# Value products of block 1's attention: both heads stationary on the full array instead of one head per half of the columns

## The chip, the cores and the metric

One core of one Trainium2 chip runs the whole program. The metric is device time in microseconds. The engines are TensorE (PE in the profile; its weight loads are listed apart as PEld), VectorE (DVE), ScalarE (ACT), GpSimd (POOL), SyncE (SP, which issues most transfers) and the DMA engines. [...]

## The reference, cut to what matters

Two transformer blocks over 1024 tokens of width 1024. The change lies in the first block's attention: 8 heads of width 64, a mixture of dilated windows.

```python
s = jnp.einsum('brnqhd,brnkhd->brnhqk', qb, kw) + bias
p = jnp.exp(s - m);  den = jnp.sum(p, -1)
o = jnp.einsum('brnhqk,brnkhd->brnqhd', p / den, vw)   # the value products
...
O = sum_i softmax(lse)_i * o_i                          # over the dilations
mix = concat(O, sgu) @ w_out
```

## The kernel before, in words

**The stage.** Block 1 has a projection part, then one `flow(gating(), attention())` call, then the output projection (`wo`) and the feed-forward layers. `flow` is a planner: it runs Python generators and decides in which order they emit their instructions, by estimated times. `gating()` is the dense stream: it makes 4 x 4 tiles `zv` and `zu` (48 matmuls of 256 columns each) and 8 tiles `mixp`. `attention()` handles head pairs j = 0 to 3: project q and k of the pair (`qk_proj`, tiles `q_p` and `k_p`, put into the dense stream), the scores of both heads (`att_scores`, tiles `spA`, `spB`), and then the value products of the pair in two halves of the tokens (`att_values(j, 0)` and `att_values(j, 1)`). The values of a pair are spawned beside the projections and scores of the next pair. A second scheduler then orders the emitted instructions on each engine by priority and by which buffers are free; each engine runs its list strictly in that order.

**A value tile.** `att_values(j, u)` makes the 128 x 512 result `oT`: 64 features of each of the two heads on the partitions, 512 tokens in the columns. It has eight steps n. In each, POOL scales the weights of both heads (`src`), PE transposes them into one bank `pt` (4 transposes of 128 columns), ACT or DVE copies the bank to `P` in SBUF, and one step later PE multiplies values by `P`. In steps 0 to 3 a step owns 128 consecutive tokens, in steps 4 to 7 every fourth token. In each step there are two halves m of the keys and two heads e, four matmuls in all:

```python
o, v = oT[ps, 128 * q:128 * q + 128], vA[:, 4 * u + q + m, ps]     # ps: 64 partitions of head e
PE.matmul(o, v, P[:, m, e, :], ...)
```

The stationary operand is 128 keys x 64 features, so a matmul takes half of the array's columns; the head picks the half. All are plain float32, which the hardware runs in two passes: each matmul of these shows as two records in the trace (the dense matmuls are float32r, one record each). At the end ACT copies `oT` to `ot` in SBUF (L689) and sends it to DRAM, from where `split_at` reads it for the output projection.

**Banks.** PSUM is split into two pools of four banks: `pg` (tag "g") for the dense stream (`zv`, `zu`, `mixp`, `q_p`, `k_p`), `psd` (tag "s") for the scores, the transposes `pt` and, before, `oT`.

Of the kernel before, what the change touches and what calls it, by code (L numbers as in the profile page):

```python
# [9 lines left out]
F32 = mybir.dt.float32  # L10
# [107 lines left out]
def tile_hybrid_two_blocks(ctx, tc, A, out, dbg=None, stop=None):  # L118
    nc = tc.nc
    dbg = dbg or {}  # L120
    PE, ACT, DVE, POOL, SP = nc.tensor, nc.scalar, nc.vector, nc.gpsimd, nc.sync
# [5 lines left out]
    pg = ctx.enter_context(tc.tile_pool(name="pg", bufs=PGB, space=PSUM))  # L127
    psd = ctx.enter_context(tc.tile_pool(name="psd", bufs=8 - PGB, space=PSUM))
# [528 lines left out]

    def att_values(j, u):

        sts = [st_of[2 * j], st_of[2 * j + 1]]  # L660
        vA, vB = vAB_of[j]
        oT = psd.tile([128, 512], F32, tag="s", name=f"oT{j}{u}")
        for n in range(9):
            if n < 8:
                i = 4 * u + n % 4
                pt = psd.tile([128, 2, 2, 128], F32, tag="s", name=f"pt{j}{u}{n}")
                for e in range(2):
                    a, b, mdA, mdB = sts[e]
                    src, md = (a[u][:, n, :], mdA) if n < 4 else (b[u][:, n - 4, :], mdB)
                    wt = md[:, 4 + i % 4 // 2, 2 * (i % 2) + i // 4:2 * (i % 2) + i // 4 + 1]  # L670
                    POOL.tensor_scalar(src, src, wt, 0.0, op0=ALU.mult, op1=ALU.add)
                    for m in range(2):
                        PE.transpose(pt[:, m, e, :], src[:, 128 * m:128 * m + 128], ident)
                P_ = p1.tile([128, 2, 2, 128], F32, tag="PT", name=f"PT{j}{u}{n}", bufs=3)
                (DVE.tensor_copy if n % 2 else ACT.copy)(P_, pt)
            if n:
                q = n - 1
                for m in range(2):
                    for e in range(2):
                        ps = slice(64 * e, 64 * e + 64)  # L680
                        if q < 4:
                            o, v = oT[ps, 128 * q:128 * q + 128], vA[:, 4 * u + q + m, ps]
                        else:
                            o, v = oT[ps, q - 4:512:4], vB[:, 4 * m + q - 4, ps]
                        PE.matmul(o, v, P[:, m, e, :], start=q == 0 and m == 0, stop=q == 7 and m == 1)
            P = P_
            yield 4 * MM, LT["vt"]
        ot = p1.tile([128, 512], F32, tag="PT", name=f"ot{j}{u}", bufs=3)
        ACT.copy(ot, oT)  # L689
        ACT.dma_start(at_d[u][j], ot)  # L690

    def attention():
        vs = []

        def first(j):
            yield 0, LT["ex"]
            yield from att_values(j, 0)

        def second(j, before):
            yield Join(before)  # L700
            yield from att_values(j, 1)

        for j in range(4):
            yield Job(qk_proj(j))
            yield 0, LT["qk"]
            for e in range(2):
                if vs:
                    yield Join(vs.pop(0))
                if e:
                    load_v(j)  # L710
                yield from att_scores(2 * j + e)
            a = yield Spawn(first(j))
            vs = [a, (yield Spawn(second(j, a)))]
        yield Join(vs[1])
# [797 lines left out]
```

## Time and profile before

| | |
|---|---|
| Time, median of 3 runs | 2614.74 us (2614.11 to 2618.09) |
| The profiled execution: time, span | 2613.16 us, 2611.2 us |
| PE busy | 2447.1 us, 94% of the span |
| PE weight loads busy | 1999.4 us, 77% |
| DVE, ACT, POOL busy | 57%, 47%, 9% |
| Mean granted PE clock, share of full | 0.971 |
| Value products (L685) on PE | 512 records, 164.1 to 429.1 us |

The share of PE is an average over the whole program, most of which is feed-forward layers. The value products of block 1 lie between 164 and 430 us, six tiles interleaved with the dense stream and two (the last pair) after it has ended. In the trace a matmul's duration contains the time that it takes to run through the array, so neighbours overlap; what a matmul costs the engine is read from the distance between starts.

### The profile page before, as it was taken

The page shows a single profiled execution, that of the slowest core. Times are in us where ns is not written, and L with a number is a line of the kernel's source. Part 1 is how long each engine was busy: PE and PEld are TensorE (multiplying, and loading weights), DVE is VectorE, ACT ScalarE, POOL GpSimd, SP SyncE. Part 2 cuts the span into 40 slices and gives each one's busy share as a digit, 9 for nine tenths or more (in the row PEclk, how much of TensorE's full clock was granted, in tenths as well). Part 3 has the DMA queues.
Part 4 walks back from the last instruction along what each step waited for, and adds up shares of the span by engine and source line. Part 5 has one row for each costly group of instructions (what it writes and reads, how often), then busy time and mean ns, then how long its engine had stood idle before and what let it go on. Part 6 is the DMA issues. An engine that isn't in the chain of part 4 may idle for free. (4 is left out here: it accounts for less than half of the span.)

```text
span 2611.2 us, 32731 instructions
## 1 busy us (share of the span) xinstructions
PE 2447.1 (94%) x12024; PEld 1999.4 (77%) x12024; DVE 1490.4 (57%) x2755; ACT 1215.4 (47%) x2160; POOL 241.5 (9%) x356
## 2 busy tenths in 40 slices
PE   8999999999999999589999999878889999799997
PEld 8867778778788788467888878667668887688886
DVE  3346444566653469476443157989996554533436
ACT  5345554463333363255545373366755443633332
POOL 1034212100000000000000000122200000100002
PEclk9999999999999999789999999989899999899998
DMA  6412114489886676346558657522222225633332
GB/s 181 120 46 64 42 30 114 161 282 325 292 269 202 218 215 223 129 138 192 165 163 273 196 158 219 173 91 81 73 81 81 81 69 164 227 97 97 97 97 73
DMA packets 330784, 391.64 MB, mean 150 GB/s; under 512 B 42273, under 2 KB 227889, under 8 KB 330624
## 3 DMA queue, kind: packets, MB, share of 16 engines
q1 hardware_dynamic: 327216, 385.11, 47.1%
q10 hardware_dynamic: 3408, 4.46, 0.5%
q8 instruction: 94, 1.54, 0.2%
q14 instruction: 66, 0.54, 0.1%
HBM read 312.44 MB, written 80.73 MB: 151 GB/s over the span
## 5 line engine op out<-in xcount | busy, mean ns | idle before, releaser
L147 PE MATMUL fb_p<-h4h,fb_w_h 128*128 128x512 f32 x512 | 205.9, 403 | 13.0 <-ACT h4h L841 8.7
L148 PE MATMUL fa_p<-h2l,fa_w_h 128*128 128x512 f32 x512 | 204.5, 399 | 0.0
L149 PE MATMUL fa_p<-h2h,fa_w_l 128*128 128x512 f32 x512 | 203.2, 397 | 0.8 <-DMA fa_w_l<-fa_w_d 0.8
L148 PE MATMUL fb_p<-h4l,fb_w_h 128*128 128x512 f32 x512 | 203.9, 399 | 0.0
L147 PE MATMUL fa_p<-h2h,fa_w_h 128*128 128x512 f32 x512 | 203.6, 398 | 0.0
L149 PE MATMUL fb_p<-h4h,fb_w_l 128*128 128x512 f32 x512 | 203.2, 397 | 0.0
L1079 DVE SCALAR_TENSOR_TENSOR y<-glu,cw,y 128x512 f32<-128x512 f32 x240 | 180.1, 790 | 1.0
L176 ACT CAST fb_w_h<-fb_w_r 128x1024 fp32r<-128x1024 f32 x64 | 67.2, 1050 | 144.0 <-PE fb1o_p L149 74.1
L147 PEld LDWEIGHTS fb_p<-h4h,fb_w_h 128*128 128x128 f32 x512 | 97.7, 191 | 34.3 <-ACT h4h L841 8.9
L1189 ACT ACTIVATE junk<-sc,cand 128x768 bf16<-128x768 f32 (+2 forms) x93 | 86.9, 934 | 62.4 <-DVE cand L1187 60.5
L148 PEld LDWEIGHTS fb_p<-h4l,fb_w_h 128*128 128x128 f32 x512 | 97.8, 191 | 20.9 <-DVE h4l L842 0.3
L149 PEld LDWEIGHTS fb_p<-h4h,fb_w_l 128*128 128x128 f32 x512 | 97.5, 190 | 20.6
L148 PEld LDWEIGHTS fa_p<-h2l,fa_w_h 128*128 128x128 f32 x512 | 96.7, 189 | 21.4 <-issue 0.9
L147 PEld LDWEIGHTS fa_p<-h2h,fa_w_h 128*128 128x128 f32 x512 | 96.3, 188 | 21.8 <-ACT fa0o_w_h L176 0.9
L149 PEld LDWEIGHTS fa_p<-h2h,fa_w_l 128*128 128x128 f32 x512 | 96.7, 189 | 21.0 <-DMA fa_w_l<-fa_w_d 1.3
L177 DVE TENSOR_TENSOR fb_w_l<-fb_w_r,fb_w_h 128x1024 fp32r<-128x1024 f32 x53 | 64.9, 1224 | 82.5 <-ACT fb_w_h L176 82.4
L1131 PE MATMUL ip<-kT,qi 128*128 128x384 f32 (+3 forms) x160 | 60.6, 421 | 51.9 <-DMA qi<-qiT_d 35.8
L1277 DVE TENSOR_TENSOR PL<-pt,PT 128x512 fp32r<-128x512 f32 (+1 forms) x80 | 50.8, 636 | 73.5 <-ACT PT L1276 73.2
L176 ACT CAST fa_w_h<-fa_w_r 128x1024 fp32r<-128x1024 f32 x32 | 33.7, 1054 | 118.4 <-PE fa0o_p L149 77.8
L1131 PEld LDWEIGHTS ip<-kT,qi 128*128 128x128 f32 x160 | 33.7, 218 | 66.7 <-DMA qi<-qiT_d 33.7
L1168 DVE TENSOR_SCALAR_CACHE_REDUCE jk<-sc,cand 128x640 bf16<-128x640 f32 (+2 forms) x93 | 81.6, 877 | 2.2
L177 DVE TENSOR_TENSOR fb1o_w_l<-fb1o_w_r,fb1o_w_h 128x1024 fp32r<-128x1024 f32 x28 | 34.3, 1225 | 83.9 <-ACT fb1o_w_h L176 83.9
(1511 smaller groups left out, 7113.4 us busy)
## 6 DMA issues: line engine op xcount, KB each, us to landing
fa_w_r<-in_w_ff_dram SPq DMA_DIRECT2D x64, 512.0 KB
fb_w_r<-in_w_up_dram SPq DMA_DIRECT2D x64, 512.0 KB
ada_w<-in_w_ada_dram SPq DMA_DIRECT2D x48, 512.0 KB
fa_w_d<-fa_w_l SPq DMA_DIRECT2D x32, 512.0 KB
fa0o_w_r<-in_w_ff_dram SPq DMA_DIRECT2D x32, 512.0 KB
fa0o_w_d<-fa0o_w_l SPq DMA_DIRECT2D x32, 512.0 KB
fa_w_l<-fa_w_d SPq DMA_DIRECT2D x32, 512.0 KB
fa1o_w_r<-in_w_ff_dram SPq DMA_DIRECT2D x32, 512.0 KB
```

The costliest lines, as they stand in the source:

```text
L147: PE.matmul(out_, lh, rh, start=first, stop=False)
L148: PE.matmul(out_, lh, rl, start=False, stop=False)
L149: PE.matmul(out_, ll, rh, start=False, stop=last)
L176: ACT.copy(hi, raw)
L177: eng.tensor_tensor(lo, raw, hi.bitcast(F32), op=ALU.subtract)
L1079: DVE.scalar_tensor_tensor(y, g, w, y, op0=ALU.mult, op1=ALU.add)
L1131: PE.matmul(p, q[:, z, 128 * j:128 * j + 128], kT[:, g, c0:c0 + m], start=z == 0, stop=z == 1)
L1168: DVE.tensor_scalar(jk[:, :ss[e].shape[-1]], ss[e], thr, 0.0, op0=op, op1=ALU.add, accum_out=cnt[:, e:e + 1])
L1189: ACT.activation(junk[:, :ss[e].shape[-1]], ss[e], AF.Sign, bias=cand[:, e:e + 1].bitcast(F32), accum_out=cnt[:, e:e + 1])
L1277: DVE.tensor_tensor(tl[:, :kk], pt[:, :kk], th[:, :kk].bitcast(F32), op=ALU.subtract)
```

## The change

`oT` becomes two banks from `pg`, each 128 x 2 x 256: partitions for the features of both heads, then a plane for each head's weights, then 256 tokens. The stationary operand is now the values of both heads (128 keys x 128 features), and the weights of both heads pass in one matmul. Half of each result is not wanted (the features of one head by the weights of the other) and is never read. In steps 0 to 3 a step has two matmuls of 256 columns; in steps 4 to 7 its tokens lie in both banks and it has four matmuls of 128 columns. The one copy at the end becomes four of 64 partitions x 256 columns that pick the wanted quarters.

```diff
-        oT = psd.tile([128, 512], F32, tag="s", name=f"oT{j}{u}")
+        oT = [pg.tile([128, 2, 256], F32, tag="g", name=f"oT{j}{u}{c}") for c in range(2)]
...
-                    for e in range(2):
-                        ps = slice(64 * e, 64 * e + 64)
-                        if q < 4:
-                            o, v = oT[ps, 128 * q:128 * q + 128], vA[:, 4 * u + q + m, ps]
-                        else:
-                            o, v = oT[ps, q - 4:512:4], vB[:, 4 * m + q - 4, ps]
-                        PE.matmul(o, v, P[:, m, e, :], start=q == 0 and m == 0, stop=q == 7 and m == 1)
+                    if q < 4:
+                        o = oT[q // 2][:, :, 128 * (q % 2):128 * (q % 2) + 128]
+                        PE.matmul(o, vA[:, 4 * u + q + m, :], P[:, m], start=q % 2 == 0 and m == 0, stop=False)
+                    else:
+                        for c in range(2):
+                            PE.matmul(oT[c][:, :, q - 4:256:4], vB[:, 4 * m + q - 4, :], P[:, m, :, 64 * c:64 * c + 64],
+                                      start=False, stop=q == 7 and m == 1)
...
-        ACT.copy(ot, oT)
+        for e in range(2):
+            for c in range(2):
+                ACT.copy(ot[64 * e:64 * e + 64, 256 * c:256 * c + 256], oT[c][64 * e:64 * e + 64, e, :])
```

The scheduler's order on PE changes little: the value products stand between the same dense matmuls. Near the start of the first value tile, where `k_p` is still being made, PE had before:

```order
L147 MATMUL k_p_1610<-h1h_1_355,k1w_h 128x512
L685 MATMUL oT_1617<-PT_1625,vAB_1251 64x128
L148 MATMUL k_p_1610<-h1l_1_357,k1w_h 128x512
L673 MATMUL pt_1652<-ident,sA_1089 128x128
L685 MATMUL oT_1617<-PT_1625,vAB_1251 64x128
L149 MATMUL k_p_1610<-h1h_1_355,k1w_l 128x512
L673 MATMUL pt_1652<-ident,sA_1089 128x128
L685 MATMUL oT_1617<-PT_1625,vAB_1251 64x128
```

and has now:

```order
L147 MATMUL k_p_1610<-h1h_1_355,k1w_h 128x512
L682 MATMUL oT_1617<-PT_1626,vAB_1251 128x2x128
L674 MATMUL pt_1651<-ident,sA_1089 128x128
L148 MATMUL k_p_1610<-h1l_1_357,k1w_h 128x512
L674 MATMUL pt_1651<-ident,sA_1089 128x128
L682 MATMUL oT_1617<-PT_1626,vAB_1251 128x2x128
L149 MATMUL k_p_1610<-h1h_1_355,k1w_l 128x512
```

One wide product stands where two narrow ones stood, still alone between dense matmuls and transposes. In steps 4 to 7 there are four products as before, also one by one; a tile has 24 product instructions now instead of 32. The other place is the second tile of pair 1, where the dense stream is at its eight `mixp` tiles (one bank each) and the scores of the next pair run. PE had before:

```order
L473 MATMUL mixp_2668<-sg,swT 128x512
L685 MATMUL oT_2631<-PT_2639,vAB_2078 64x128 [waits Activation_49]
...
L473 MATMUL mixp_2842<-sg,swT 128x512
L673 MATMUL pt_2671<-ident,sA_2102 128x128 [waits Pool_49]
L473 MATMUL mixp_2855<-sg,swT 128x512
L608 MATMUL spA_0_2698<-kH_2334,q_2332 128x192 [waits PE_49]
L673 MATMUL pt_2671<-ident,sA_2102 128x128
L473 MATMUL mixp_2922<-sg,swT 128x512 [waits Activation_49]
```

and has now:

```order
L682 MATMUL oT_2619<-PT_2628,vAB_2070 128x2x128 [waits Activation_49]
L473 MATMUL mixp_2655<-sg,swT 128x512 [waits PE_49]
...
L682 MATMUL oT_2620<-PT_2665,vAB_2070 128x2x128 [waits Activation_49]
L473 MATMUL mixp_2826<-sg,swT 128x512 [waits PE_49]
L473 MATMUL mixp_2839<-sg,swT 128x512
```

Both banks of `oT` are taken early, and the fourth `mixp` moves back behind five score blocks: fewer dense matmuls are left to fill this tile.

## Rows read from the trace of the kernel before

**Rows 1.** The page, busy time of PE over the span

```profile
PE 2447.1 (94%) x12024; PEld 1999.4 (77%) x12024; DVE 1490.4 (57%) x2755; ACT 1215.4 (47%) x2160; POOL 241.5 (9%) x356
```

**Rows 2.** Windows of six value stretches: length; PE, PEld, DVE, ACT, POOL busy; clock

```profile
164.08:188.80 24.72, 24.72 (x150) 16.47 (x149) 6.54 (x9) 6.72 (x11) 3.81 (x7) 1.00 0.11 33
188.80:207.87 19.07, 18.96 (x145) 14.16 (x144) 12.36 (x40) 9.59 (x26) 2.31 (x7) 1.00 0.02 4
245.88:275.80 29.92, 29.92 (x151) 19.21 (x151) 8.10 (x12) 7.43 (x12) 6.42 (x9) 0.83 0.09 28
275.80:295.60 19.80, 19.78 (x132) 12.78 (x131) 8.83 (x36) 16.02 (x42) 0.82 (x3) 1.00 0.05 7
327.93:353.40 25.47, 25.47 (x151) 16.59 (x150) 6.49 (x11) 5.83 (x10) 2.40 (x4) 1.00 0.03 11
353.40:373.65 20.25, 20.02 (x132) 13.44 (x131) 7.61 (x27) 10.40 (x26) 0.00 (x0) 1.00 0.02 1
```

**Rows 3.** Timeline of PE, a value product alone between dense matmuls

```profile
171.46 0.43 PE L685 MATMUL oT<-PT,vAB 128*64 128x128 f32 x2
171.82 0.39 PE L147 MATMUL zv<-zv_w_h,h1h 128*128 128x256 f32 x1
172.05 0.27 PE L673 MATMUL pt<-ident,sB 128*128 128x128 f32 x1
172.25 0.43 PE L685 MATMUL oT<-PT,vAB 128*64 128x128 f32 x2
```

**Rows 4.** Timeline of PE, prices of neighbours and of four products in a run

```profile
405.05 0.28 PE L148 MATMUL zu<-zu_w_l,h1h 128*128 128x256 f32 x1
405.17 0.28 PE L149 MATMUL zu<-zu_w_h,h1l 128*128 128x256 f32 x1
...
195.49 0.60 PE L673 MATMUL pt<-ident,sB 128*128 128x128 f32 x4
...
188.84 0.66 PE L685 MATMUL oT<-PT,vAB 128*64 128x128 f32 x8
```

**Rows 5.** Timeline of weight loads, a value product and its neighbours

```profile
164.98 0.19 PEld L685 LDWEIGHTS oT<-PT,vAB 128*64 128x64 f32 x2 [0.27 <-issue]
165.35 0.19 PEld L149 LDWEIGHTS k_p<-h1h,k1w_l 128*128 128x128 f32 x1 [0.17 <-issue]
165.48 0.14 PEld L673 LDWEIGHTS pt<-ident,sA 128*128 128x128 f32 x1
```

**Rows 6.** Full-array float32 matmuls: timeline of PE, and the instructions of mixp

```profile
279.18 0.28 PE L673 MATMUL pt<-ident,sA 128*128 128x128 f32 x1
279.29 1.02 PE L473 MATMUL mixp<-sg,swT 128*128 128x512 f32 x2
...
L473 PE MATMUL mixp<-sg,swT x16: 591/592/697, 274.9 to 297.0; 128*128 128x512 f32 x16
```

**Rows 7.** Windows, oT's instructions alone: length; PE, PEld, ACT busy; clock

```profile
164.08:188.80 24.72, 11.47 (x64) 5.44 (x64) 0.59 (x1) 1.00 0.11 33
188.80:207.87 19.07, 7.77 (x64) 4.21 (x64) 0.00 (x0) 1.00 0.02 4
245.88:275.80 29.92, 12.97 (x64) 6.14 (x64) 0.59 (x1) 0.83 0.09 28
275.80:295.60 19.80, 7.12 (x64) 4.04 (x64) 0.00 (x0) 1.00 0.05 7
327.93:353.40 25.47, 11.47 (x64) 5.44 (x64) 0.59 (x1) 1.00 0.03 11
353.40:373.65 20.25, 9.92 (x64) 4.91 (x64) 0.00 (x0) 1.00 0.02 1
408.00:429.30 21.30, 10.81 (x128) 7.75 (x128) 0.58 (x1) 1.00 0.23 75
```

**Rows 8.** Copies out of PSUM on ACT, lengths in ns by column count

```profile
L1276 ACT CAST PT<-pt x80: 351/586/590, 1123.5 to 2168.8; 128x512 fp32r<-128x512 f32 x64, 128x256 fp32r<-128x256 f32 x16
```

**Rows 9.** Waits of PE between 140 and 435 us: total, times, longest

```profile
PE oT L685 <- ACT PT L675: 4.4, 3, 2.6
```

## What was predicted

> **What bounds the kernel now.** I began with the page: PE is busy for 94% of the span [rows 1]. That is a mean over a program that is mostly feed-forward layers, so I cut out the stage of the change by windows, one for each value tile of pairs 0 to 2. In these six stretches PE is busy practically all the time (24.72 of 24.72 us, 18.96 of 19.07, and so on), while ACT is busy for a quarter to a half of them, except in the fourth (16.02 of 19.80), and DVE and POOL less than two thirds [rows 2]. PE is the bound there, and everything behind it in its list moves with it. Over the whole stage PE waits little for what the value products need: 4.4 us in three waits, the longest 2.6 us [rows 9].
>
> Next I read what a value product costs PE, from distances between starts. A dense matmul of 256 columns starts 0.12 us after the last [rows 4]. Four transposes last 0.60 us and one 0.27 us, so a further one costs (0.60 - 0.27)/3 = 0.11 us [rows 3, 4]. From one lone value product to the next there are 172.25 - 171.46 = 0.79 us, and between them stand one dense matmul and one transpose [rows 3]. So a lone product costs 0.79 - 0.12 - 0.11 = 0.56 us. Its two passes of 128 columns should cost 2 x 0.11 = 0.22 us by the transposes. The other 0.34 us is what I take the change to be about.
>
> Where it lies is seen in the weight loads: the load for a product idles 0.27 us before it and starts with the product itself, and the load of the dense matmul behind it idles 0.17 us, while the transpose after that shows no gap [rows 5]. Going from the full array to half of its columns and back, PE neither loads nor multiplies ahead. That plain float32 among float32r is not the reason is seen in `mixp`, which is float32 on the full array: it starts 0.11 us behind a transpose [rows 6].
>
> The half-array form has its merit too: four products in a run last 0.66 us where one lasts 0.43 [rows 3, 4], so three more cost only 0.23 us. The two heads pass at the same time in their halves. But most stand alone, since the scheduler puts a dense matmul or a transpose between them.
>
> [...]
>
> **The change, part by part.**
>
> *The products, after.* `mixp` gives the price of float32 on the full array: two passes of 512 columns last 1.02 us and one 0.59, so a pass takes 0.43 us, 0.215 for 256 columns, and 0.11 for 128 [rows 6]. A product of 256 columns in two passes costs 0.43 us, one of 128 columns 0.22 us. A tile has 8 of the first and 16 of the second: 3.44 + 3.52 = 7.0 us. No mode changes, so I add no gap.
>
> *The products, before.* The busy time of `oT`'s instructions is 11.47, 7.77, 12.97, 7.12, 11.47 and 9.92 us in the six stretches [rows 7]. Each run of products costs 0.56 - 0.43 = 0.13 us more than its busy time, which is a factor of 1.30 for one alone and 0.79/0.66 = 1.20 for four. The first tile of each pair has nearly all of them alone: I take 1.27, so 14.6, 16.5 and 14.6, together 45.7 us. The second tiles have more runs, and I take 1.20: 9.3, 8.5 and 11.9, together 29.7 us. The sum is 75.4 us.
>
> *Difference in the six tiles.* After, 6 x 7.0 = 42.0 us, and 1.4 us more in the third stretch, whose granted clock is 0.83 [rows 2]: 43.4 us. PE saves 32.0 us.
>
> *The last pair* has no dense stream beside it, and its products stand in long runs: 10.81 us busy [rows 7], with a factor of 1.1 (an estimate from 0.13 us a run, which is less beside longer runs) 11.9 us. After, 14.0 us. This costs 2.1 us, since no dense work is left behind which it could hide.
>
> *The copies.* Four copies of 256 columns instead of one of 512. On ACT a copy out of PSUM takes 351 ns for 256 columns and 586 for 512 [rows 8]; a tile so costs 4 x 0.35 - 0.59 = 0.8 us more of ACT. I cost this at nothing: ACT has 9 us or more to spare in five of the six stretches [rows 2]. Without that cover it would be 8 x 0.8 = 6.5 us. Behind the first copy on ACT stand the next tile's copies of `pt` and the evictions of the dense tiles; they wait 0.8 us longer, and PE has a dense tile to go on with.
>
> *The banks.* The dense stream has two banks instead of four while a value tile runs, and the transposes and scores have four instead of three. A dense tile `zv` needs 48 x 0.12 = 5.8 us of PE, and its eviction is one ACT instruction of a copy's size, so one bank filling and one emptying do; costed at nothing, and the price if it fails is the first rival. The fourth bank for the transposes is costed at nothing as well.
>
> *What does not come through.* Where the second tile of a pair runs beside the next pair's scores, ACT and DVE have work of their own. In the fourth stretch ACT is at 81%, and the dense `mixp` moves back: I count none of the 1.5 us there. In the second and sixth, ACT is at half and I count three quarters of 7.2 us. That takes off 1.5 + 1.8 = 3.3 us.
>
> *Sum.* -32.0 + 2.1 + 3.3 = -26.6 us. PE is as busy behind the stage as in it [rows 1], so I let this through to the end. The profiled execution took 2613.16 us and the median of the runs shown is 2614.74, 1.6 us above; so 2614.7 - 26.6 = 2588 us.
>
> *Bounds.* Lower: factor 1.30 in all six (60.72 us busy becomes 78.9), 42.0 after, the last pair free: -37, 2578 us. Upper: the first tiles gain only on their busy time (35.9 - 22.4 = 13.5), the second ones nothing, the last pair costs 2.1: -11.4, 2603 us.
>
> **The rivals.**
>
> *Only part of it.* Score chain and copies take over as soon as PE gets faster, in the second tiles wholly and in the first ones partly: -11 to -20 us, 2595 to 2604. For it: PE's list is fixed, and in the fourth stretch ACT is nearly full. Against it: in the first tiles ACT is busy for 6.7 of 24.7 us. Chance 0.24.
>
> *The dense stream stalls on a bank (slower).* The place is the first matmul of a `zv`, `zu` or `mixp` tile while `oT` holds two of four banks. In the third stretch the trace shows what a stall does: PE waited 2.6 us [rows 9], and then had a granted clock of 0.83 over 29.9 us [rows 2], which is 0.17 x 29.9 = 5.1 us. A stall of that size in each of six tiles costs 6 x 7.7 = 46 us: 2634 us. It decides from 26.6/6 = 4.4 us per tile on. For it: the changed order puts a wait ahead of `mixp`. Against it: evictions are ten times shorter than the filling of a tile. Chance 0.06.
>
> *The gap stays.* If PE loses 0.34 us at each value product for another reason, the 92 runs that the changed order has in the six tiles (124 before) lose 31 us, and with 42 us of passes that is 73 us against 75: no change, 2615 us after the last pair. Against it: the start of `mixp` [rows 6]. Chance 0.05.
>
> *Passes count, gaps do not (slower).* If most of the gap were covered now, only the passes would count: a step's four products take 0.43 us in halves and 0.86 us after, 64 steps, +27 us, 2641 us. Against it: 0.79 us from start to start with 0.45 us of passes between [rows 3]. [...] Chance 0.03.
>
> **How the numbers follow.** The forecast, a gain of 20 to 37 us, has 0.62; its own range is 2578 to 2595 us, the likeliest 2588. The range for 8 in 10 takes in the forecast and the partial case: 2577 to 2604. About 0.2% (5 us) can be told from no change. Faster by more: 0.62 and nearly all of 0.24, 0.85. Within: the rest of that and most of the third rival, 0.05. Slower: 0.10.
>
> **What would show it.** In the profile after, a value product on the full array should have a start-to-start share of 0.43 or 0.22 us, with no idle time ahead of its weight load; the records should be 384 instead of 512; the first stretch, now 24.7 us from the first product of one tile to that of the next, should take about 17, and the second, fourth and sixth 15 to 20 instead of 19 to 20. The first `wo` matmul should come some 26 us earlier, and the time from there to the end should stay. I am wrong if weight loads still idle around the products, if PE idles for microseconds ahead of dense tiles, or if the granted clock falls in more stretches than the third.

## The result, and the profile after

The changed kernel takes 2587.79 us (median of 4 runs, 2585.66 to 2589.95), the kernel before on the same chip 2614.43 us (4 runs, 2613.11 to 2618.09): a ratio of 0.9898, 95% interval 0.9882 to 0.9913, or some 27 us less. Forecast were 2588 us and a range of 2577 to 2604.

The page of the changed kernel, busy time of the engines over the span; it answers to [rows 1]. PE has 128 records fewer and 26 us less of busy time, and its share of the span stays at 94%:

```profile
PE 2420.8 (94%) x11896; PEld 2010.4 (78%) x11896; DVE 1490.0 (58%) x2755; ACT 1221.3 (47%) x2184; POOL 236.3 (9%) x356
```

Where did the time go? Two rows of PE's timeline tell where to look, the first matmul of the output projection in the kernel before and in the changed one:

```profile
431.01 0.48 PE L147 MATMUL wo_p<-wo_w_h,sgH 128*128 128x512 f32 x1
```

```profile
402.72 0.48 PE L147 MATMUL wo_p<-wo_w_h,sgH 128*128 128x512 f32 x1
```

It comes 28.3 us earlier. The span is 2611.2 - 2585.5 = 25.7 us shorter, so from there to the end the changed kernel takes 2.6 us more. That is not the change: in the profiles of the kernels below this remainder lies between 2179 and 2185 us, whatever was edited ahead of it. The whole gain lies in the stage of block 1.

Windows of the changed kernel: the six value stretches, cut as in [rows 2], then the three stretches between pairs and the last pair up to the first `wo` (length; PE, PEld, DVE, ACT, POOL busy; clock, DMA share, GB/s):

```profile
162.88:180.59 17.71, 17.67 (x134) 16.51 (x133) 8.03 (x10) 7.54 (x14) 4.53 (x9) 1.00 0.14 45
180.59:197.60 17.01, 16.04 (x121) 14.70 (x119) 11.93 (x38) 10.29 (x30) 2.21 (x5) 1.00 0.03 9
240.51:258.20 17.69, 17.69 (x134) 16.53 (x133) 6.59 (x9) 7.07 (x13) 3.89 (x7) 1.00 0.14 45
258.20:277.40 19.20, 19.07 (x115) 14.86 (x114) 9.19 (x35) 15.84 (x41) 0.96 (x3) 1.00 0.03 5
310.95:329.18 18.23, 18.23 (x135) 17.01 (x134) 6.49 (x11) 6.71 (x13) 2.46 (x4) 1.00 0.04 16
329.18:343.94 14.76, 14.56 (x111) 13.45 (x110) 7.36 (x25) 10.36 (x26) 0.00 (x0) 1.00 0.00 1
...
197.60:240.51 42.91, 38.18 (x217) 32.87 (x215) 30.90 (x104) 26.43 (x66) 20.72 (x43) 0.92 0.33 82
277.40:310.95 33.55, 33.53 (x184) 27.79 (x183) 16.37 (x75) 21.35 (x58) 18.76 (x36) 1.00 0.28 71
343.94:380.29 36.35, 35.41 (x295) 34.86 (x294) 20.25 (x86) 27.44 (x69) 17.28 (x37) 1.00 0.29 76
380.29:402.72 22.43, 22.01 (x162) 19.61 (x161) 8.08 (x11) 9.26 (x19) 0.00 (x0) 1.00 0.30 95
```

The last four of these in the kernel before, same columns:

```profile
207.86:245.88 38.02, 34.95 (x205) 30.05 (x205) 28.05 (x100) 25.91 (x66) 19.58 (x39) 1.00 0.35 94
295.59:327.93 32.34, 32.34 (x178) 27.00 (x178) 15.70 (x73) 19.82 (x53) 19.02 (x36) 1.00 0.29 72
373.64:408.03 34.39, 33.46 (x277) 32.91 (x276) 19.62 (x82) 26.45 (x64) 18.83 (x36) 1.00 0.30 79
408.03:431.01 22.98, 20.51 (x205) 15.86 (x205) 9.85 (x14) 8.76 (x15) 1.36 (x2) 1.00 0.27 86
```

Against [rows 2] the six value stretches are 7.0, 2.1, 12.2, 0.6, 7.2 and 5.5 us shorter, 34.6 together. The three stretches between them are 4.9, 1.2 and 2.0 us longer, 8.1 together. The last pair is 0.5 us shorter, and the first tile begins 1.2 us earlier. The sum, -34.6 + 8.1 - 0.5 - 1.2 = -28.2, is the 28.3 us of the `wo` matmul.

A value product itself is seen in PE's timeline after, as in [rows 3]:

```profile
168.32 0.28 PE L148 MATMUL zv<-zv_w_l,h1h 128*128 128x256 f32 x1
168.44 0.60 PE L682 MATMUL oT<-PT,vAB 128*128 128x256 f32 x2
168.87 0.27 PE L674 MATMUL pt<-ident,sB 128*128 128x128 f32 x1
...
172.27 0.38 PE L685 MATMUL oT<-PT,vAB 128*128 128x128 f32 x2
172.49 0.27 PE L674 MATMUL pt<-ident,sB 128*128 128x128 f32 x1
```

From the product's start to the next matmul's are 0.43 us at 256 columns and 0.22 at 128, and the product starts 0.12 us behind the dense matmul ahead of it, as a further dense matmul would. In the weight loads the idle times of [rows 5] are nearly gone:

```profile
163.65 0.30 PEld L682 LDWEIGHTS oT<-PT,vAB 128*128 128x128 f32 x2
163.98 0.19 PEld L149 LDWEIGHTS k_p<-h1h,k1w_l 128*128 128x128 f32 x1
```

Added up between 140 and 435 us, idle time ahead of a product's weight load that nothing in the profile explains ("issue": total, times, longest) was 13.7 us in the kernel before and is 1.5 us in the changed one:

```profile
PEld oT L685 <- issue: 13.7, 56, 0.8
```

```profile
PEld oT L682 <- issue: 1.0, 4, 0.2
PEld oT L685 <- issue: 0.5, 2, 0.2
```

### The profile page after: what moved, and what is told of

Its sections match the earlier page's. It is cut to its first block, busy times and chain, and to the rows that moved or that the text cites. A ratio compares the mean times of both kernels' runs of the same rounds, so it can differ in the third digit from the quotient of the medians.

```text
span 2585.5 us, 32503 instructions
## 1 busy us (share of the span) xinstructions
PE 2420.8 (94%) x11896; PEld 2010.4 (78%) x11896; DVE 1490.0 (58%) x2755; ACT 1221.3 (47%) x2184; POOL 236.3 (9%) x356
## 4 chain that ended last, share of the span: by engine, by line
PE 60%; DVE 13%; DMA 11%; issue 10%; ACT 4%; POOL 2%; SPq 1%; POOLq 0%; ACTq 0%; DVEq 0%
DMA qi<-qiT_d 3%; PE fa_p L149 3%; PE fa_p L147 3%; PE fa_p L148 3%; PE fb_p L147 3%; PE fb_p L148 3%; PE fb_p L149 3%; DVE y L1082 3%; PE fa0o_p L148 2%; PE fa0o_p L149 2%; PE fa0o_p L147 2%; PE fb1o_p L147 2%; PE fb1o_p L149 2%; PE fb1o_p L148 2%; DVE jk L1171 2%
## 5 line engine op out<-in xcount | busy, mean ns | idle before, releaser
L1134 PEld LDWEIGHTS ip<-kT,qi 128*128 128x128 f32 x160 | 34.6, 223 | 64.0 <-DMA qi<-qiT_d 30.1
```

Of the source, the lines that this page charges most:

```text
L1134: PE.matmul(p, q[:, z, 128 * j:128 * j + 128], kT[:, g, c0:c0 + m], start=z == 0, stop=z == 1)
```

## The experiments

The theory: a run of half-array products costs some 0.34 us for going from the full array to half of it and back (the change of mode), and the change gains since it takes these gaps away. Rivals: the gain comes from the banks that the transposes and scores get; or a value product costs something fixed, and there are fewer of them. In the trace before, the 256 products stand in 135 runs, 103 of them of one product; in the one after, the 192 products stand in 107.

**The half array, products kept together.** The products of the kernel before, unchanged, but no other matmul may be put between the four of a step: 68 runs instead of 135 (52 were expected). PE's later instructions in the program are made to follow the step's last product: a change of order in PE's list.

```diff
+    class Fenced:
...
+        def _after(self):
+            i = nc.cur_bb.bb.instructions[-1]
+            if self.mark is not None and i.engine == self.mark.engine:
+                tc.add_manual_dep(i, self.mark.name, mybir.DependencyInfo(
+                    mybir.DependencyClass.NoSync, mybir.DependencyReason.DATA), reason="behind the step's products")
...
+        def matmul(self, *a, **k):
+            nc.tensor.matmul(*a, **k)
+            self._after()
...
+    PE = Fenced()
...
                         PE.matmul(o, v, P[:, m, e, :], start=q == 0 and m == 0, stop=q == 7 and m == 1)
+                PE.mark = nc.cur_bb.bb.instructions[-1]
```

> The half-array products of before, but the four of a step kept together by ordering edges on PE (52 runs of products instead of 135; the transposes of a step come together too). If the cost of before is the change between half and full array, paid once for each run: 48 steps in the six tiles at 0.79 us are 38 us instead of 75, so about as fast as the changed kernel or faster, 2578 to 2592 us. If the full-array form itself is what helps (fewer or wider instructions, other banks), this stays at 2610 to 2620 us.

Measured: 2584.44 us, before 2612.91, ratio 0.9898 (0.9876 to 0.9921). The gain is that of the change, with the old form, the old bank and the old copy. PE's timeline of this kernel, where four products stand between transposes and dense matmuls:

```profile
171.96 0.60 PE L137 MATMUL pt<-ident,sA 128*128 128x128 f32 x4
172.49 0.66 PE L133 MATMUL oT<-PT,vAB 128*64 128x128 f32 x8
173.07 0.39 PE L133 MATMUL zv<-zv_w_h,h1h 128*128 128x256 f32 x1
173.30 0.28 PE L133 MATMUL zv<-zv_w_l,h1h 128*128 128x256 f32 x1
...
174.42 0.66 PE L133 MATMUL oT<-PT,vAB 128*64 128x128 f32 x8
```

From the start of these four to the start of the next four are 174.42 - 172.49 = 1.93 us, and between them stand six dense matmuls and four transposes. Less 6 x 0.12 and 4 x 0.11 us that is 0.77 us a step. On the full array a step costs 2 x 0.43 = 0.86, and alone in halves 4 x 0.56 = 2.24.

**The half array in pairs.** The same, but only two products kept together, so that 119 runs are left.

```diff
+                    PE.mark = nc.cur_bb.bb.instructions[-1]
+                    if n:
+                        products(n - 1, e, P)
...
+            PE.mark = nc.cur_bb.bb.instructions[-1]
```

(`products` makes the two heads' products of one half of the keys.)

> The half-array products of before, kept together in pairs instead of fours: between the two pairs of a step stand the two transposes of one head, with ordering edges on PE. 119 runs of products by its order, where the fours have 68. If each change to half of the array and back costs 0.34 us, the 51 further runs cost 17 us: 2598 to 2606 us, between the fours (2584) and before (2613). If keeping the products behind each other matters for another reason (fewer stalls of the order as such), the edges alone give the gain: 2582 to 2590 us.

Measured: 2604.13 us, before 2611.69, ratio 0.9965 (0.9953 to 0.9976). The interval is 6 to 12 us. The gain grows with the number of runs that are taken away: 16 fewer gave 7.6 us, 67 fewer gave 28.5, which is 0.47 and 0.42 us a run. That is more than the 0.34 of the gap, and a run of two shows why. From one step to the next in this kernel's timeline, two runs, six dense matmuls and four transposes start:

```profile
172.09 0.44 PE L133 MATMUL oT<-PT,vAB 128*64 128x128 f32 x4
...
174.31 0.44 PE L133 MATMUL oT<-PT,vAB 128*64 128x128 f32 x4
```

A run of two takes (2.22 - 6 x 0.12 - 4 x 0.11)/2 = 0.53 us, no more than the 0.56 of a lone product, so joining two lone products saves the gap and a product's passes. Not all of it reaches the time. In this execution the granted clock was 0.50 for 13.65 us in the second value tile, where the kernel before had 1.00 [rows 2] (window; columns as above):

```profile
193.00:206.65 13.65, 13.50 (x62) 9.75 (x63) 5.12 (x22) 6.32 (x21) 1.28 (x5) 0.50 0.18 46
```

That cost 0.5 x 13.50 = 6.8 us. So the order of the three kernels is shown, and the price of a run by this one only as 0.4 to 0.8 us (its interval over 16 runs).

**The bank alone.** The kernel before, with its one `oT` bank taken from the dense pool.

```diff
-        oT = psd.tile([128, 512], F32, tag="s", name=f"oT{j}{u}")
+        oT = pg.tile([128, 512], F32, tag="g", name=f"oT{j}{u}")
```

> The half-array products of before with their one bank taken from the dense pool; nothing else. If the change between half and full array is the cost, the 123 runs in the six tiles (124 before) still pay it: 2609 to 2619 us. If freeing a bank for transposes and scores is what helped, this gets a good part of the gain: 2590 to 2603 us.

Measured: 2611.73 us, before 2612.91, ratio 0.9993 (0.998 to 1.0006). No change. PE's timeline of this kernel has the lone product as it was, 0.36 us to the start of the next matmul, as in [rows 3]:

```profile
166.46 0.43 PE L685 MATMUL oT<-PT,vAB 128*64 128x128 f32 x2
166.82 0.50 PE L147 MATMUL k_p<-h1h,k1w_h 128*128 128x512 f32 x1
```

**The full array with the banks of the scores' pool.** The changed kernel with both banks from there: the dense stream keeps its four, transposes and scores are left two.

```diff
-        oT = [pg.tile([128, 2, 256], F32, tag="g", name=f"oT{j}{u}{c}") for c in range(2)]
+        oT = [psd.tile([128, 2, 256], F32, tag="s", name=f"oT{j}{u}{c}") for c in range(2)]
```

> The full-array products of the change with their two banks from the pool of the scores and transposes, so that these have two left. By the change of mode as the cost it keeps most of the gain, less what two banks cost the transposes and scores: 2586 to 2600 us. If the banks of the dense pool are needed for the gain: above 2605 us.

Measured: 2588.98 us, before 2612.91, ratio 0.9913 (0.9888 to 0.9938). The gain stays, whichever pool gives the banks. That rules the banks out as its source.

**The full array, one bank for each head.** As many products as before (32 a tile, of 128 columns) and two copies instead of four, but every product on the full array.

```diff
+                    for e in range(2):
+                        if q < 4:
+                            o, v = oT[e][:, 128 * q:128 * q + 128], vA[:, 4 * u + q + m, :]
+                        else:
+                            o, v = oT[e][:, q - 4:512:4], vB[:, 4 * m + q - 4, :]
+                        PE.matmul(o, v, P[:, m, e, :], start=q == 0 and m == 0, stop=q == 7 and m == 1)
```

> Full array, one bank for each head's weights: 32 products of 128 columns in a tile instead of 8 of 256 and 16 of 128, the same columns in all, two copies at the end instead of four. If a full-array product costs its passes alone: 2584 to 2592 us, as the changed kernel. If each product instruction carries a fixed cost of some 0.3 us whatever its form: 64 more of them cost about 20 us, 2605 to 2610 us.

Measured: 2590.04 us, before 2612.91, ratio 0.9916 (0.9893 to 0.9939). The 64 products more than in the changed kernel cost nothing that the runs can tell (the intervals overlap), and at 0.3 us each it would be 19 us: what counts is the form.

**The full array, products kept together.** The changed kernel with the ordering of the first experiment.

```diff
+                PE.mark = nc.cur_bb.bb.instructions[-1]
```

> The full-array products of the change, with the same ordering edges as the fours. A full-array product has no change of mode to share, so keeping them together should give nothing: within 5 us of the changed kernel, 2584 to 2593 us. If the edges themselves help, as a better order, 2575 to 2582 us.

Measured: 2591.53 us, before 2611.69, ratio 0.9926 (0.9904 to 0.9948). Keeping products together is worth 28 us where they change the mode, and nothing where they don't: this kernel is 20 us faster than the kernel before, the changed kernel 24 to 27. This is the sharpest evidence for the gap.

**The cast behind the scaling.** In the changed kernel PE waits 4.7 us in the first stretch between pairs (below), and ahead of the scaling for which it waits, POOL does a cast for a later product. Here the cast is queued behind it.

```diff
-        POOL.tensor_copy(qB.rearrange("p (r t) -> p r t", r=4), q2.rearrange("p (t r) -> p r t", r=4))
+        with tc.issue_after(scaled[0]) if scaled[0] else ExitStack():
+            POOL.tensor_copy(qB.rearrange("p (r t) -> p r t", r=4), q2.rearrange("p (t r) -> p r t", r=4))
...
+                    scaled[0] = nc.cur_bb.bb.instructions[-1]
```

> The changed kernel with the 2.0 us cast of qB on POOL queued behind the scaling of the pair before. In the changed kernel that cast moved ahead of the scaling of pair 1, PE then waits 4.7 us instead of 2.6 for the first transposed tiles, and a small DVE instruction of the softmax chain lasts 1.94 us beside the cast instead of 0.16. If the cast is what gives a part of the gain back: 2 to 4 us faster than the changed kernel, 2583 to 2586 us. If the chain is late by the exchange of the maxima ahead of it in any case: no change, 2586 to 2590 us.

Measured: 2586.13 us, before 2611.69, ratio 0.9902 (0.9885 to 0.992). The time doesn't tell it from the changed kernel. PE's waits in that stretch, in the changed kernel and in this one:

```profile
PE pt L674 <- POOL sA L672: 4.7, 1, 4.7
```

```profile
PE pt L677 <- POOL sA L674: 3.2, 1, 3.2
```

The cast made 1.5 us of the wait at most; where the rest comes from was not tried.

**Both, on the half array.** Products kept together and the cast queued late, as in the first and the last experiment.

> The fours of half-array products with the same late cast. In the fours' own profile the cast already stands mostly behind the scaling, so this should change nothing: 2581 to 2588 us. If the two gains add up, 2578 to 2582 us.

Measured: 2580.81 us, before 2611.69, ratio 0.9881 (0.9863 to 0.9899). That lies in the range for two gains that add up, but only 0.2 us below the other one. So I ran it again, beside the changed kernel on one chip:

> The changed kernel itself, on the same chip as the next one, so that the two can be set side by side: ratio to before 0.988 to 0.991.

> Fours of half-array products with the late cast, on the same chip as the changed kernel. The fours cost 0.79 us a step, the full array 0.86 to 0.88; over 64 steps that is 4 to 6 us. If that is what tells them apart: 3 to 8 us faster than the changed kernel. If the earlier 2581 us was the chip's: within 2 us of it.

Measured: the changed kernel 2587.28 us (2584.82 to 2587.7), ratio 0.9897 (0.9881 to 0.9914); the half array with products together and the late cast 2581.88 us (2580.76 to 2583.48), ratio 0.988 (0.9865 to 0.9895); before 2611.51. The second is 5.4 us faster, and no run of the one lies among those of the other. It is the fastest version found. How much of the 5.4 us is the grouping and how much the cast wasn't separated. The two profiled executions, 6.4 us apart, place less than a third of it in the stage of the change: the first value product starts at 161.71 us against 163.79 (2.1 us), from there to the first `wo` matmul are 237.99 us against 239.76 (1.8), and the remainder is 2179.3 us against 2181.9 (2.6), within the spread of remainders above.

## Why the prediction was right, step by step

**The mode change, from the full array to half of it and back, was the cost.** Point by point the products came out as forecast: 0.43 and 0.22 us a product, 384 records, 1.5 us of unexplained idle time ahead of their weight loads instead of 13.7. The runs show more than the trace could: the gain is there without the new form (products together), absent with the new bank alone, and larger the more runs are taken away. The rivals "the gap stays" and "passes count, gaps do not" are out. The size of the gap is measured, 0.34 us at a lone product and 0.42 to 0.47 us for each run taken away; why PE doesn't load or multiply ahead there, the 0.27 us of [rows 5], no run here shows. Where products stand together the halves are worth something too, though little: 0.77 us a step against 0.86. Less the gap of 0.34 us, paid once a run, that leaves an estimated 0.43 us of passes, half of the full array's and what the last rival assumed; the gap takes most of it back. One argument of the forecast showed less than it was put for: the transpose ahead of `mixp` is plain float32 too (`ident` and `sA` are float32 tiles), so that row can't rule out a cost of float32 among float32r. The row after the change does: on the full array a float32 product starts 0.12 us behind a float32r `zv`.

**The first tiles: 7.6 us each forecast (14.6 - 7.0), 7.0 and 7.2 measured** in the first and fifth stretch, each with as many other records as before (86 and 87: [rows 2], less the 64 or 48 of `oT`). PE's list was fixed, and everything in it moved up, as argued. "Only part of it" did not happen here.

**The third tile: the clock was charged in the wrong place.** I left the granted clock of 0.83 in this stretch and added 1.4 us for it, so the forecast was 16.5 - 7.0 - 1.4 = 8.1 us. The clock is 1.00 after, and the stretch is 12.2 us shorter: 7.1 us as in its sisters, and 0.17 x 29.92 = 5.1 us from the clock. But the low clock has only moved. Finer windows of the kernel before show it (columns as above):

```profile
240.00:245.88 5.88, 2.98 (x15) 2.07 (x16) 4.50 (x7) 2.92 (x5) 5.88 (x12) 0.99 0.40 124
245.88:250.00 4.12, 4.12 (x11) 2.08 (x12) 1.45 (x3) 0.58 (x1) 4.12 (x7) 0.50 0.00 0
250.00:260.00 10.00, 10.00 (x48) 6.60 (x47) 3.19 (x4) 3.32 (x6) 2.30 (x4) 0.70 0.18 55
```

And of the changed kernel:

```profile
226.00:232.00 6.00, 4.61 (x21) 3.34 (x19) 5.60 (x18) 2.69 (x6) 0.54 (x1) 1.00 0.57 165
232.00:236.00 4.00, 0.67 (x2) 0.53 (x3) 3.91 (x7) 0.93 (x2) 2.65 (x4) 0.71 0.09 17
236.00:240.51 4.51, 4.51 (x15) 3.33 (x13) 2.54 (x5) 2.33 (x4) 4.51 (x11) 0.50 0.35 115
```

In both, PE idles for the weights of the new pair (2.9 us before, 4.7 after), and then runs at a granted clock of 0.50 (4.12 us of it in the second window above, 4.51 us in the last one here). Before, the slow time fell into the value tile, where PE was busy throughout; after, it falls ahead of it and partly into the wait itself, where it costs nothing. PE worked 0.67 + 4.51 = 5.2 us of it, half of which, 2.6 us, is lost. Another 1.7 us of the 4.9 that this stretch is longer are PE's idle time (42.91 - 38.18 = 4.7 us after, 38.02 - 34.95 = 3.1 before). Taken together the clock gave 5.1 - 2.6 = 2.5 us. That PE's wait is longer after was not foreseen. A part of it is the cast on POOL; why the exchange of maxima ahead of it comes later, measured from the tile's end, was not tried.

**The second tiles: 5.4 us forecast (1.7, 0 and 3.7), 8.2 measured** (2.1, 0.6, 5.5). I took off 3.3 us as not coming through. But part of the extra is work put off, as PE's records of a single tile name show, in the stretches between pairs of the kernel before (`zv`, `mixp`, `pt` in this order, and `pt` in the last pair too: length, PE busy, clock, DMA share, GB/s):

```profile
207.86:245.88 38.02, 10.92 (x67) 1.00 0.35 94
...
295.59:327.93 32.34, 1.98 (x4) 1.00 0.29 72
...
373.64:408.03 34.39, 1.04 (x8) 1.00 0.30 79
408.03:431.01 22.98, 8.30 (x56) 1.00 0.27 86
```

And in the changed kernel:

```profile
197.60:240.51 42.91, 11.99 (x74) 0.92 0.33 82
...
277.40:310.95 33.55, 2.74 (x6) 1.00 0.28 71
...
343.94:380.29 36.35, 2.40 (x20) 1.00 0.29 76
380.29:402.72 22.43, 7.58 (x46) 1.00 0.30 95
```

The shorter tiles end before 7 `zv` and 2 passes of `mixp` come up, and the next stretch has them: 7 x 0.12 + 2 x 0.43 = 1.7 us by the prices of the forecast. The 12 further `pt` come from the other side: the tile ahead has its 24 as before, and the last pair, whose row closes each list, has 46 instead of 56 (two stand across the cut and count in both). They are 12 x 0.11 = 1.3 us of the last pair's work, done earlier. With the clock's 2.6 us and the longer wait's 1.7 that is 7.3 of the 8.1 us by which these stretches grew. The forecast had nothing for them: what comes through was looked for in each tile, not in the stretch that follows it.

**The last pair: +2.1 us forecast, -0.5 measured.** This term had the wrong sign. The passes are there: `oT`'s busy time rose from 10.81 [rows 7] to 16.53 us. But "no dense work is left behind which it could hide" overlooked that PE idled there: 22.98 - 20.51 = 2.5 us before and 22.43 - 22.01 = 0.4 after. In this stage, which waits for its chain, the extra passes fell into the waits. Ten of the pair's transposes were also done earlier (56 records before, 46 after), which takes 1.1 us off this term and adds them to the stretch ahead.

**What was costed at nothing.** The copies took 367 ns instead of the estimated 351, 32 of them, and no wait of PE names them. On the banks, the ratios with either pool are 0.9898 and 0.9913, with intervals that overlap. "The dense stream stalls on a bank" left one mark: 0.2 us that a weight load of `mixp` waited once for a copy of `oT`.

**The sum** was met by terms that miss to both sides:

| us | forecast | measured |
|---|---|---|
| first tiles of pairs 0 to 2 | -23.3 | -26.4 |
| second tiles | -5.4 | -8.2 |
| last pair | +2.1 | -0.5 |
| stretches between the pairs | 0 | +8.1 |
| start of the first tile | 0 | -1.2 |
| to the first `wo` matmul | -26.6 | -28.2 |

Three terms gained 8.5 us more than forecast, and the stretches that had no term gave 8.1 back. Both come mostly from the same three things: the slow time that moved out of the third tile, dense work put off, and transposes done earlier. Each leaves one row of the table for another, so the misses nearly cancel; the forecast saw none of the three. That the mechanism was the gap is shown by the experiments; that the total came out so close to 2588 us is partly luck. The first tile's earlier start is no effect of the change that could be told: the changed kernel run again has its first product at 163.79 us instead of 162.88.

## What to carry to other kernels

Read what a small matmul costs from start to start, with its neighbours, not from its duration: here a dense matmul of 256 columns lasts 0.28 us and the next one starts after 0.12, and three fifths of a lone product's 0.56 us stood in the gaps around it. The half-array products paid here where the four of a step stood in a run, 0.77 us a step against 0.86 on the full array; alone between full-array matmuls they cost 2.24 us. Where a scheduler separates such products, either keep the run together or pass twice the columns on the full array. Before charging extra work to a stage without cover, look whether its engine idles there; and when a stage gets shorter, look for the work that it covered in the stage behind it.

## What the hardware showed that was not expected

A small operation on DVE lasted 1.94 us, twelve times as long as its sister's 0.16. POOL's timeline in the changed kernel, and then DVE's:

```profile
231.46 2.00 POOL L601 CAST qB<-q 128x1024 fp32r<-128x1024 f32 x1 [8.83 <-DVE q L540]
234.80 1.85 POOL L672 TENSOR_SCALAR sA<-sA,mdA 128x256 f32<-128x256 f32 x4 [1.35 <-DVE mdB L654]
```

```profile
230.51 0.16 DVE L653 TENSOR_TENSOR mdA<-mdA,otA 128x8 f32<-128x8 f32 x1
...
231.54 1.94 DVE L653 TENSOR_TENSOR mdB<-mdB,otB 128x8 f32<-128x8 f32 x1
```

The operation for head B starts 0.08 us after POOL's cast and ends with it (233.48 and 233.46), while the same one for head A takes 0.16 us. With the cast queued late it takes 0.12. The two ends agree to 0.02 us; what ties the one to the other, no run here shows. POOL's scaling waits for what DVE makes of `mdB` next, 1.35 us after the cast in the row above, so by these rows the cast keeps it back on its own queue and, if it is what holds DVE, through DVE too.

The half array with products together should beat the full array by 0.86 - 0.77 = 0.09 us a step, some 6 us over 64 steps. Without the late cast no difference is seen (both ratios are 0.9898, with intervals 8 and 12 us wide, in which 6 us could hide); with it there are 5.4 us, of which the profiles place only 1.8 between the first value product and the first `wo` matmul. The waits of PE in the kernel with products together point to where the rest may have gone: 8.8 us in six waits ahead of products, for ACT's copies of `pt`. The same view of the changed kernel has none ahead of its products.

```profile
PE oT L133 <- ACT PT L694: 8.8, 6, 5.5
```

The kernel with the late cast has the same waits (8.8 us in six), so they are not what the late cast took away. All this is argued from views, not tried.
